# A decoder layer in split fp32: moving operands shifted by 128 bytes against the weights

## The chip, the cores and the metric

The kernel runs on one core of one Trainium2 chip. The metric is the device time of one execution in microseconds (us). Differences below about 0.2% of the time (4 us) can't be told from none.

## The reference

One layer of a hybrid decoder on 512 tokens of width 2,048, followed by a final norm:

```python
h = rms_norm(x, mix_norm_g)
p = h @ w_in                                   # 2048 -> 5136
out_a = conformer_conv_group(...)              # GLU, causal conv of width 31, LayerNorm, SiLU, 1024 x 1024
out_b = gated_deltanet_group(...)              # 8 value heads of 128, gated delta rule in chunks
x = x + concatenate([out_a, out_b]) @ w_out    # 2048 -> 2048
h = rms_norm(x, ffn_norm_g)
gate, up = split(h @ w_up, 2)                  # 2048 -> 2 x 5632
gate = causal_depthwise_conv(gate, ffn_conv_w) + ffn_conv_b
x = x + (silu(gate) * up) @ w_down             # 5632 -> 2048
return rms_norm(x, final_norm_g)
```

All inputs and outputs are float32.

## The kernel before

**Split products.** Activations lie transposed: 128 channels on the partitions, the 512 tokens along the free axis. The large products run in the type fp32r. Each operand is split in two tiles, a rounded high part (hi) and the remainder (lo). `mm3` (line 490) then issues three matmuls for a weight slice of 128 x 128: hi weights by hi activations, hi weights by lo activations, lo weights by hi activations. The stationary operand (`lhsT`, here called the weights) is loaded anew for every matmul, and TensorE loads the next one while the current moving operand (`rhs`, the activations) streams. Weights come from HBM in raw blocks of 128 x 1024 (`load_next`, line 450); ACT rounds 512 columns of one to hi (a cast), DVE subtracts to get lo (`split_piece`, line 460). A piece (hi, lo) holds four slices, 512 bytes apart within its 2,048 bytes.

**Stages.** The input projections come first, from the operands `xgh` and `xgl`, with the attention and convolution chains in between: small fp32 matmuls, transposes (`tr`), and the decay products `dec<-slgh,upper_r`. Then the mixer's output projections: `obh`, `obl` by half of `w_out`, `yh`, `yl` by the pointwise weights, `ah`, `al` by the other half. Then the FFN's up stage: 44 blocks, each of which computes the gate and up columns of 128 channels in seven products of half the tokens and half the depth instead of eight (a Strassen-like scheme). Its moving operands are `xb` (in the tiles XB) and `xt` (in XT), 256 columns each; DVE adds and subtracts raw weight blocks for it. Every second weight piece of the up stage is called `uhi`, `ulo`, the others `whi`, `wlo` (`cast`, line 1397). Last comes the down stage, with the stored FFN activations loaded again and split to `dh` and `dl`; its last tile runs in two halves of 256 tokens, with split weights in the tiles of `DT`.

**Order.** The order on every engine is written out by a planner in the program (class `Flow`): it keeps a clock for each engine from fixed costs of operations by shape, and starts tasks when their inputs are due by it. The address of a tile plays no part in it.

**Where tiles lie.** SBUF is given out from both ends. From the left: constants (`const`), the weight pool `wts` (three raw blocks, four hi and four lo pieces), then, one stage after another, the attention tiles, `xb`, `xt` and the down operands. From the right: the pool `pad` with one tile of 480 words that nothing uses (lines 314 and 315), then `acts1` and `acts2` (the split activations of the input and output projections), `conf`, and later in the same space `halves` (which prepares the up operands), `up` (line 1367: raw blocks `uraw`, `uhi`, `ulo`, and the small tiles of the FFN's output path) and `down2`. All tiles of weights and moving operands are multiples of 1 KB in size, so what lies ahead of the first tile of a side sets where all of them begin within 2 KB. `upper_r`, the weights of the decay products, is allocated after some small tiles and so begins elsewhere: at a multiple of 512 bytes.

Of the kernel before, what the change touches and what calls it, by code (L numbers as in the profile page):

```python
# [14 lines left out]
F32 = mybir.dt.float32  # L15
BF16 = mybir.dt.bfloat16
F32R = mybir.dt.float32r
# [4 lines left out]
P = 128  # L22
# [284 lines left out]
def tile_trunk(ctx: ExitStack, tc: tile.TileContext, xT, w_k, w_ba, w_m, pw, w_out, w_up, w_down, par_d, cst_d, out):  # L307
    nc = tc.nc
    fl = Flow(nc)
    V, ACT, POOL, SP = fl.vector, fl.scalar, fl.gpsimd, fl.sync  # L310
    ctx.enter_context(tc.manual_schedule(engines=ENGINES))
    cpool = ctx.enter_context(tc.tile_pool(name="const", bufs=1))
    wpool = ctx.enter_context(tc.tile_pool(name="wts", bufs=1))
    pad = ctx.enter_context(tc.tile_pool(name="pad", bufs=1, side="right"))
    pad.tile([P, 480], F32, name="pad")
    actx, a2ctx, cctx, gctx = [ExitStack() for _ in range(4)]
    apools = [
        c.enter_context(tc.tile_pool(name=n, bufs=1, side="right", reuse_waits="tile"))
# [9 lines left out]
    def nm(s):  # L328
        uid[0] += 1
        return f"{s}_{uid[0]}"  # L330

    def A(name, second=False):
        return fl.tile(apools[second], [P, T], F32R, "a", KT, nm(name))
# [116 lines left out]
    def load_next():  # L450
        i = len(raws)
        if i < (len(plan) if up_done else up_at + 3):
            src, n, step = plan[i]
            raw = fl.tile(wpool, [P, 1024], F32, "raw", 3, nm("wraw"))
            for o in range(0, n, n if i else step):
                e = o + (n if i else step)
                SP.dma_start(raw[:, o:e], src[:, o:e])
            raws.append(raw)
# [103 lines left out]
    def split_scaled(src, g, name, alloc):  # L562
        hi = alloc(name + "h")
        lo = alloc(name + "l")
        ACT.activation(out=hi, in_=src, func=AF.Copy, scale=g)
        V.scalar_tensor_tensor(out=lo, in0=src, scalar=g, in1=hi.bitcast(F32), op0=ALU.mult, op1=ALU.subtract)
        return hi, lo
# [97 lines left out]
    for k in range(KT):  # L665
# [4 lines left out]
        hi, lo = split_scaled(xs, mix_g[:, k : k + 1], "xg", lambda n: A(n, k >= KH))  # L670
# [566 lines left out]
    octx, xctx, tctx, uctx = [ExitStack() for _ in range(4)]  # L1237
# [21 lines left out]
    for m in range(NC):  # L1259
        ps = mtile(yhl)  # L1260
        hi, lo = A("ah"), A("al")
# [102 lines left out]
    fl.spawn(rms_stats(total[0], rstd2, 3.0), 6.0)  # L1364
    tctx.close()
    actx.close()
    upool = uctx.enter_context(tc.tile_pool(name="up", bufs=1, side="right", reuse_waits="tile"))

    def U(tag, bufs, w=T, dt=F32):
        return fl.tile(upool, [P, w], dt, tag, bufs, nm(tag))  # L1370

    def products_of(f):
        return PRODUCTS[0 if f == 0 else 2 if f == NF - 1 else 1]

    def up_products():


        blocks = {}

        def load(f, *names):  # L1380
            for n in names:
                if f == NF:
                    if n in (11, 22):
                        up_done.append(True)
                        load_next()
                    continue
                i, j = n // 10 - 1, n % 10 - 1
                if n in (11, 22):
                    t = fl.tile(wpool, [P, 1024], F32, "raw", 3, nm("wraw"))
                else:  # L1390
                    t = U("uraw", 3, 1024)
                SP.dma_start(t, w_up[2 * f + i][:, j * 1024 : (j + 1) * 1024])
                blocks[f, n] = t

        pend = deque()

        def cast(t, o):
            if o:
                hi, lo = U("uhi", 4, 512, F32R), U("ulo", 4, 512, F32R)
            else:  # L1400
                hi, lo = [fl.tile(wpool, [P, 512], F32R, n, 4, nm("w" + n)) for n in ("hi", "lo")]
            src = t[:, o * 512 : o * 512 + 512]
            ACT.copy(out=hi, in_=src)
            pend.append((src, hi, lo))

        def low():
            src, hi, lo = pend.popleft()
            V.tensor_tensor(out=lo, in0=src, in1=hi.bitcast(F32), op=ALU.subtract)
            pieces.append((hi, lo))

        def combine(out, a, b, op=ALU.subtract):
            V.tensor_tensor(out=out, in0=a, in1=b, op=op)

        blocks.update({(0, n): raws[up_at + i] for i, n in enumerate((11, 12, 22))})
        load(0, 21)

        def steps(f, a11, a22, a12, a21):

            def start():
                load(f + 1, 21)  # L1420
                if f:
                    load(f + 1, 11)

            def s1():
                combine(a22, a21, a22, ALU.add)

            def s2():
                combine(a22, a22, a11)
                load(f + 1, 22 if f else 11)

            def s3():
                combine(a21, a11, a21)

            def s4():
                combine(a12, a12, a22)

            if f in (0, NF - 1):
                start()
                urgent.extend((s1, s4))
                units = {  # L1440
                    "22": (a22, None, s1), "s1": (a22, s3, lambda: combine(a22, a22, a11)), "s3": (a21, None, None),
                    "s2": (a22, None, None), "11": (a11, None, lambda: load(NF, 22)), "12": (a12, None, s4),
                    "s4": (a12, None, None)}
                if f == 0:
                    units["s1"] = (a22, s3, s2)
                    units["s3"] = (a21, lambda: combine(a12, a12, a22), lambda: load(1, 12))
                    units["s2"] = (a22, None, lambda: load(1, 22))
            else:
                units = {
                    "11": (a11, start, None), "22": (a22, None, s1), "12": (a12, s3, None), "s1": (a22, None, s2),  # L1450
                    "s3": (a21, s4, lambda: load(f + 1, 12)), "s2": (a22, None, None if f else lambda: load(1, 22)),
                    "s4": (a12, None, None)}
            return [units[n] for n in products_of(f)]

        then, urgent = None, []
        for f in range(NF):
            units = steps(f, *[blocks.pop((f, n)) for n in (11, 22, 12, 21)])
            if f == 0:
                units = units[2:]
            for t, *acts in units:  # L1460
                for o in (0, 1):
                    if then in urgent:
                        low()
                        then()
                        then = None
                        yield
                    cast(t, o)
                    yield
                    if len(pend) > 1:
                        low()  # L1470
                    if then:
                        then()
                        yield
                    then = acts[o]
        low()
        load_next()
# [69 lines left out]
    for f in range(NF):  # L1546
# [7 lines left out]
        for n, w in enumerate(products_of(f)):  # L1554
            b, c, x = products[w]
            for k in range(KH):
                if k % 4 == 0:
                    hi, lo = pieces.popleft()
# [216 lines left out]
```

## Time and profile before

| | us |
|---|---|
| median of 3 runs | 2167.09 |
| lowest, highest | 2165.31, 2169.3 |
| the profiled execution's own time | 2161.55 |
| its span, first to last instruction | 2159.8 |

The profile shows one execution. Share of the span in which an engine is busy: TensorE's matmuls 99%, its weight loads (which run beside them) 89%, DVE 75%, ACT 44%, GpSimd 3%. The mean granted clock of TensorE is 0.997 of full speed. Matmuls overlap in the records: a record lasts from the issue to the last result, so its duration is longer than the time until the next one begins. The pace is read from the starts, or from a piece of the chain of waits, which gives the time and the number of matmuls that follow each other without a gap.

### The profile page before, as it was taken

To read this page: it belongs to the slowest core of one execution; us is meant where nothing else is said; L and a number is where in the kernel's file an instruction comes from. 1 tells how busy PE (TensorE), PEld (TensorE's weight loads), DVE (VectorE), ACT (ScalarE), POOL (GpSimd) and SP (SyncE) were. 2 spreads that over 40 slices of the span, in tenths; PEclk is the share of its full clock that TensorE was granted. 3 is DMA by queue.
4 is the path that set the end of the run, shared out by engine and by line. 5 is a ranking of instruction groups with operands and counts; after the bars stand their busy time and mean duration, and the time that the engine had idled before them with its cause. 6 is when DMAs were issued, how large, how long until landed. Compare 5 with 4: busy or idle time off the path is not lost.

```text
span 2159.8 us, 34257 instructions
## 1 busy us (share of the span) xinstructions
PE 2139.0 (99%) x13340; PEld 1926.0 (89%) x13340; DVE 1625.2 (75%) x2692; ACT 953.8 (44%) x1672; POOL 60.6 (3%) x59
## 2 busy tenths in 40 slices
PE   9999999999999999999999999999999999999997
PEld 7888888888788889999999999999999888888886
DVE  6899778888834789999999999999998633344344
ACT  5643544443333554554455455445445422233232
POOL 0310011000000000000000000000000000000000
PEclk9999999999999999999999999999999999999998
DMA  5252333333553533333343343343343733343333
GB/s 199 92 163 98 117 105 107 112 104 126 191 194 132 193 128 128 123 121 110 123 127 104 123 131 103 120 131 108 114 132 128 258 110 120 107 142 91 99 100 111
DMA packets 117618, 276.63 MB, mean 128 GB/s; under 512 B 23376, under 2 KB 36304, under 8 KB 117456
## 3 DMA queue, kind: packets, MB, share of 16 engines
q1 hardware_dynamic: 117312, 274.45, 39.5%
q8 instruction: 104, 1.70, 0.3%
q14 instruction: 58, 0.48, 0.1%
q10 hardware_dynamic: 144, 0.01, 0.0%
HBM read 240.33 MB, written 34.08 MB: 127 GB/s over the span
## 4 chain that ended last, share of the span: by engine, by line
PE 93%; DVE 3%; DMA 1%; issue 1%; ACT 0%; SPq 0%; POOLq 0%; POOL 0%; DVEq 0%; ACTq 0%
PE acc L99 49%; PE bz L99 11%; PE by L99 11%; PE bx L99 11%; PE bv L99 6%; PE tr L99 1%; DVE cacc L99 1%; DVE wlo L99 1%; PE e L99 1%; DMA wraw<-in_w_down_dram 0%; DMA yr<-scr_y 0%; PE pv L99 0%; PE ba L99 0%; PE po L99 0%; PE y L99 0%
## 5 line engine op out<-in xcount | busy, mean ns | idle before, releaser
L99 DVE TENSOR_TENSOR wlo<-wraw,whi 128x512 fp32r<-128x512 f32 (+1 forms) x616 | 414.3, 676 | 321.3 <-ACT whi L99 320.9
L99 ACT CAST whi<-wraw 128x512 fp32r<-128x512 f32 (+1 forms) x616 | 370.0, 606 | 579.1 <-PE acc L99 424.1
L99 PE MATMUL acc<-dh,wlo 128*128 128x512 f32 (+1 forms) x726 | 277.9, 383 | 0.8 <-DVE wlo L99 0.8
L99 PE MATMUL acc<-dh,whi 128*128 128x512 f32 (+1 forms) x726 | 278.0, 383 | 0.2 <-ACT whi L99 0.2
L99 PE MATMUL acc<-dl,whi 128*128 128x512 f32 (+1 forms) x726 | 277.9, 383 | 0.1
L99 PE MATMUL acc<-xgh,whi 128*128 128x512 f32 x640 | 260.2, 407 | 0.9 <-ACT xgh L99 0.9
L99 PE MATMUL acc<-xgl,whi 128*128 128x512 f32 x640 | 249.8, 390 | 0.6 <-DVE xgl L99 0.6
L99 PE MATMUL acc<-xgh,wlo 128*128 128x512 f32 x640 | 250.3, 391 | 0.0
L99 DVE SCALAR_TENSOR_TENSOR cacc<-u,par,cacc 128x495 f32<-128x495 f32 (+22 forms) x240 | 173.4, 741 | 1.7 <-ACT cacc L99 0.3
L99 PEld LDWEIGHTS acc<-dh,wlo 128*128 128x128 f32 x726 | 136.4, 188 | 27.8 <-DVE wlo L99 1.2
L99 PEld LDWEIGHTS acc<-dl,whi 128*128 128x128 f32 x726 | 136.4, 188 | 27.1 <-DVE dl L99 0.5
L99 PEld LDWEIGHTS acc<-dh,whi 128*128 128x128 f32 x726 | 136.4, 188 | 27.0 <-ACT whi L99 0.6
L99 ACT CAST uhi<-wraw 128x512 fp32r<-128x512 f32 x176 | 109.2, 621 | 104.2 <-PE by L99 64.8
L99 ACT CAST whi<-uraw 128x512 fp32r<-128x512 f32 x130 | 80.7, 621 | 151.6 <-DVE uraw L99 86.7
L99 PEld LDWEIGHTS acc<-xgh,wlo 128*128 128x128 f32 x640 | 120.1, 188 | 26.2
L99 DVE TENSOR_TENSOR ulo<-wraw,uhi 128x512 fp32r<-128x512 f32 x176 | 120.7, 686 | 28.8 <-ACT uhi L99 28.8
L99 PEld LDWEIGHTS acc<-xgh,whi 128*128 128x128 f32 x640 | 120.4, 188 | 24.3 <-ACT xgh L99 1.8
L99 PEld LDWEIGHTS acc<-xgl,whi 128*128 128x128 f32 x640 | 120.5, 188 | 23.3 <-DVE xgl L99 1.2
L99 PE MATMUL by<-xt,whi 128*128 128x256 f32 x704 | 130.5, 283 | 0.0
L99 PE MATMUL by<-xt,uhi 128*128 128x256 f32 x704 | 130.5, 283 | 0.0
L99 PEld LDWEIGHTS by<-xt,whi 128*128 128x128 f32 x704 | 109.8, 192 | 0.0
L99 PEld LDWEIGHTS by<-xt,uhi 128*128 128x128 f32 x704 | 109.8, 192 | 0.0
(277 smaller groups left out, 4722.0 us busy)
## 6 DMA issues: line engine op xcount, KB each, us to landing
wraw<-in_w_up_dram SPq DMA_DIRECT2D x89, 512.0 KB, 4.5
uraw<-in_w_up_dram SPq DMA_DIRECT2D x87, 512.0 KB, 4.4
wraw<-in_w_m_dram SPq DMA_DIRECT2D x74, 512.0 KB, 3.5
wraw<-in_w_down_dram SPq DMA_DIRECT2D x60, 512.0 KB, 3.6
wraw<-in_w_out_dram SPq DMA_DIRECT2D x32, 512.0 KB, 3.7
wraw<-in_w_down_dram SPq DMA_DIRECT2D x30, 384.0 KB, 3.4
scr_a<-fa SPq DMA_DIRECT2D x44, 256.0 KB, 2.1
dl<-scr_a SPq DMA_DIRECT2D x44, 256.0 KB, 5.1
```

What stands on the lines that cost most here:

```text
L99: return f(**kw) if not args else f(out, *args, **{k: v for k, v in kw.items() if k != "out"})
```

## The change

Three edits, all of them to where tiles lie. A pool `lpad` of one tile of 32 words (128 bytes) stands on the left, behind the weight pool, so every tile on the left after the weights begins 128 bytes later. The pad on the right shrinks from 480 to 448 words, so every tile on the right begins 128 bytes later too. In the up stage a further pad of 32 words and a pool `upw` stand on the right ahead of `up`: `uhi` and `ulo` get their tiles there and keep their start within 2 KB, and the rest of `up` lies below them.

```diff
@@ -311,8 +311,10 @@
     ctx.enter_context(tc.manual_schedule(engines=ENGINES))
     cpool = ctx.enter_context(tc.tile_pool(name="const", bufs=1))
     wpool = ctx.enter_context(tc.tile_pool(name="wts", bufs=1))
+    lpad = ctx.enter_context(tc.tile_pool(name="lpad", bufs=1))
+    lpad.tile([P, 32], F32, name="lpad")
     pad = ctx.enter_context(tc.tile_pool(name="pad", bufs=1, side="right"))
-    pad.tile([P, 480], F32, name="pad")
+    pad.tile([P, 448], F32, name="pad")
     actx, a2ctx, cctx, gctx = [ExitStack() for _ in range(4)]
@@ -1364,6 +1366,9 @@
     tctx.close()
     actx.close()
+    upad = uctx.enter_context(tc.tile_pool(name="upad", bufs=1, side="right"))
+    upad.tile([P, 32], F32, name="upad")
+    uwpool = uctx.enter_context(tc.tile_pool(name="upw", bufs=1, side="right", reuse_waits="tile"))
     upool = uctx.enter_context(tc.tile_pool(name="up", bufs=1, side="right", reuse_waits="tile"))
@@ -1396,7 +1401,7 @@
         def cast(t, o):
             if o:
-                hi, lo = U("uhi", 4, 512, F32R), U("ulo", 4, 512, F32R)
+                hi, lo = [fl.tile(uwpool, [P, 512], F32R, n, 4, nm("u" + n)) for n in ("hi", "lo")]
             else:
                 hi, lo = [fl.tile(wpool, [P, 512], F32R, n, 4, nm("w" + n)) for n in ("hi", "lo")]
```

## Rows read from the trace of the kernel before

**Rows 1.** Busy us by stage: window, length, PE, PEld, DVE, ACT, POOL, clock, DMA, GB/s.

```profile
60.00:545.00 485.00, 485.00 (x2492) 404.80 (x2491) 414.60 (x839) 225.62 (x421) 53.58 (x47) 1.00 0.36 115
...
601.30:769.80 168.50, 168.50 (x745) 139.53 (x744) 95.06 (x158) 74.00 (x131) 0.00 (x0) 1.00 0.51 169
769.80:1624.60 854.80, 852.03 (x7098) 851.59 (x7098) 783.43 (x1146) 427.44 (x725) 1.39 (x1) 1.00 0.37 119
...
1685.70:2137.80 452.10, 452.10 (x2035) 376.08 (x2036) 183.81 (x287) 137.80 (x240) 0.00 (x0) 1.00 0.38 117
```

**Rows 2.** The chain that ended last, shares of the span by engine.

```profile
PE 93%; DVE 3%; DMA 1%; issue 1%; ACT 0%; SPq 0%; POOLq 0%; POOL 0%; DVEq 0%; ACTq 0%
```

**Rows 3.** Groups of matmuls by form: out<-in, shape, count, busy us, mean ns, idle before.

```profile
L99 PE MATMUL acc<-dl,whi 128*128 128x512 f32 x682 | 265.5, 389 | 0.1
...
L99 PE MATMUL acc<-xgh,wlo 128*128 128x512 f32 x640 | 250.3, 391 | 0.0
...
L99 PE MATMUL by<-xt,whi 128*128 128x256 f32 x704 | 130.5, 283 | 0.0
...
L99 PE MATMUL acc<-obh,wlo 128*128 128x512 f32 x128 | 49.8, 389 | 0.0
...
L99 PE MATMUL acc<-ah,whi 128*128 128x512 f32 x128 | 49.8, 389 | 0.0
...
L99 PE MATMUL acc<-yh,whi 128*128 128x512 f32 x64 | 24.9, 389 | 0.0
```

**Rows 4.** Pieces of the chain of waits: start us, us, engine, tile, matmuls.

```profile
601.32 168.71 PE acc L99 x744
...
1005.46 5.76 PE by L99 x48
```

**Rows 5.** PE in order of time, around a pair of decay products: start us, us.

```profile
112.91 0.39 PE L99 MATMUL acc<-xgl,whi 128*128 128x512 f32 x1
113.13 0.40 PE L99 MATMUL acc<-xgh,wlo 128*128 128x512 f32 x1
113.37 0.39 PE L99 MATMUL dec<-slgh,upper_r 128*128 128x512 f32 x1
113.60 0.39 PE L99 MATMUL dec<-slgl,upper_r 128*128 128x512 f32 x1
113.83 0.40 PE L99 MATMUL acc<-xgh,whi 128*128 128x512 f32 x1
114.07 0.39 PE L99 MATMUL acc<-xgl,whi 128*128 128x512 f32 x1
```

**Rows 6.** PE in order of time, first and eleventh product after transposes.

```profile
162.09 0.40 PE L99 MATMUL acc<-xgl,whi 128*128 128x512 f32 x1
...
164.40 0.39 PE L99 MATMUL acc<-xgh,wlo 128*128 128x512 f32 x1
```

**Rows 7.** PE in order of time, bf16 warm-up, two overlapping windows.

```profile
4.50 1.03 PE L99 MATMUL warm<-wz 128*128 128x512 bf16 x4
...
4.93 0.59 PE L99 MATMUL warm<-wz 128*128 128x512 bf16 x2
```

**Rows 8.** PE in order of time, thirteen fp32 products of 64 columns.

```profile
238.22 1.61 PE L99 MATMUL e<-yt,DEm 128*128 128x64 f32 x13
```

**Rows 9.** The same products by tile: ns minimum/median/maximum, first and last start.

```profile
L99 PE MATMUL e<-yt,DEm x16: 218/275/275, 237.9 to 239.6; 128*128 128x64 f32 x16
```

**Rows 10.** Busy us in one block of the up stage, columns as in rows 1.

```profile
1005.46:1025.62 20.16, 20.16 (x170) 20.16 (x170) 18.50 (x29) 10.09 (x18) 0.00 (x0) 1.00 0.36 118
```

**Rows 11.** ACT and DVE in order of time at the start of the up stage.

```profile
775.37 1.23 DVE L99 TENSOR_TENSOR xt<-d,xt 128x1024 fp32r<-128x1024 f32 x1 [0.78 <-ACT xt L99]
...
776.59 0.61 ACT L99 CAST uhi<-wraw 128x512 fp32r<-128x512 f32 x1
...
783.18 0.37 ACT L99 COPY s<-bx 128x256 f32<-128x256 f32 x1
```

## The prediction

> **What bounds the kernel now.** I read the stage table first [rows 1]. In the input projections (60 to 545 us), the mixer's output projections (601 to 770), the FFN's up stage (770 to 1625) and its down stage (1686 to 2138) TensorE is busy for all but 3 us, with a granted clock of 1.00, which is the 2.4 GHz level. DVE, next after PE and its weight loads, is busy for 783 of 855 us in the up stage and less elsewhere. The chain of waits agrees: 93% of it is PE [rows 2]. So the time is the number of matmuls times the gap between their starts, and only a change in that gap can matter.
>
> The counts come from rows and code. Full-width products (512 moving columns): three per weight slice, so 3 x (682 + 640 + 128 + 128 + 64) = 4,926 [rows 3]. Half-width products of the up stage: 44 blocks x 7 products x 8 slices x 3 = 7,392, of which one operand pair makes 704 [rows 3]. Left out are 132 half-width products of the last down tile, 32 of the beta/decay projection and 16 of the decay matrices, discussed below.
>
> The gaps come from the chain [rows 4]. In the up stage 48 matmuls take 5.76 us: 120.0 ns each. In the output projections 744 take 168.71 us: 226.8 ns. The difference of 106.8 ns is for 256 more columns, 0.417 ns a column, so both shapes carry the same fixed part: 120.0 - 106.8 = 13 ns. 7,392 x 120.0 + 4,926 x 226.8 = 887 + 1,117 = 2,004 us of the 2,159.8 us span, and the fixed part alone is 12,318 x 13 ns = 160 us of it. That is what the change can touch.
>
> **The change, part by part.** The instructions, their order and their tiles' sizes stay: the planner's times in the code don't depend on addresses. No copy, load, wait or matmul is added or taken away.
>
> *Where the operands stand.* Summing the pools' sizes puts every weight tile 96 bytes past a multiple of 2 KB, on both sides of memory. A product's weights are a slice that starts 0, 512, 1,024 or 1,536 bytes into it. Moving tiles now also start 96 past, so modulo 512 bytes moving operand and weights start together. Afterwards the moving ones start at 224, the weights stay at 96. Exempt are the three groups above: the last down tile's split weights share a pool with the moving operands and shift with them, as do the padded beta/decay weights, and the decay products keep the distance they have.
>
> *What the distance does to the gap.* The trace of before has almost one distance only, so this is bounded from the nearest rows. Steps of 512 bytes are free: the 48 matmuls of one chain piece use slices at all four starts, at 120.0 ns throughout [rows 4]. A distance of 96 bytes is not free. The decay products take weights (upper_r) that start at a multiple of 512 while the stream beside them starts 96 later; from the last ordinary product before them to the second one after them four gaps take 0.94 us [rows 5], where four steady ones take 4 x 0.2268 = 0.907: 8 ns more each. The gap also isn't fixed at equal distance: after an interruption by transposes, ten gaps take 2.31 us [rows 6], 231 ns, before they settle at 227. So the fixed part depends on how the two streams meet. Ends of the range: above, 8 ns x 12,318 = +99 us. Below, two rows show shorter fixed parts: bf16 products of 512 columns, which repeat one set of weights, start 0.43 us apart for two [rows 7], 215 ns, 11.8 less; and fp32 products with only 64 moving columns but a full weight load each start (1.61 - 0.275) / 12 = 111 ns apart [rows 8, 9], so a load can come every 111 ns, 9 less than 120. That gives -(11.8 x 4,926 + 9 x 7,392) = -58 - 67 = -125 us. I take 0 between the ends, by the row nearest to it in kind: whatever in the pattern repeats must do so within 512 bytes and not within 32, since 96 is a multiple of 32 and costs something. That leaves 64, 128, 256 or 512, and at the first two a shift of 128 changes nothing.
>
> The Trainium skill ("TensorE: Matmul & The Clock Gate", Part 2, on loading the stationary operand) says that PE has two independent SBUF read ports and that loading the next weights does not steal read bandwidth from a running matmul; by it the change is worth 0. The rows of the decay products speak against that rule in general: there a different start of the weights goes with 8 ns a gap.
>
> *The split weights' own pool.* On the right uhi and ulo move to the top, over tiles of the attention and convolution operands, the rest of the up pool below them; the raw blocks stay. The first uhi is written at 776.59 us, behind whi on ACT [rows 11], and the tiles now under it had their last matmul before 770. The small tiles now over the buffers of halves are written from 783.18 us on, after the last xt, which DVE ends at 776.6 [rows 11]. Cost 0; if such a wait did come, it would be within the 3 us for which PE already stands idle there, and of that size.
>
> *Sum.* 2,161.6 us for the profiled execution (span 2,159.8 plus 1.8) + 0 + 0 = 2,161.6. The median of the three runs shown is 5.5 higher, 2,167.1, so I forecast 2,167.
>
> **The rivals.** *Faster: the streams stop meeting.* For it: the fixed part is the same 13 ns at 256 and 512 columns, as a collision that happens once per weight load would be, and equal starts are where two readers should collide most. Against it: no row at another distance has a shorter gap with weights of this type. In full it is worth -125 us by the rows, 2,042; but DVE would then have to do its 18.50 us of a block [rows 10] while PE needs 168 x 111 ns = 18.6 us, so the up stage would stand at DVE's edge and I hold about 110 of it for reachable: 2,057. Half a collision less gives 2,112.
>
> The skill's page gives a gap of columns / 2.4 plus about 2.5 ns for a warm stream (same page, "Back-to-back issue gap"). By it an estimate would be 10.8 ns x 12,318 = 133 us less, 2,034; the measured 120 and 226.8 ns already stand 11 ns above that rule.
>
> *Slower: the new distance is a worse meeting.* One mechanism: the stream begins 128 bytes ahead of the weights and runs into them later in the load, as in the decay products. Its place is every ordinary product, its price 4 ns a gap (as after an interruption: 231 - 226.8) to 8 ns (decay products), so +52 to +99 us: 2,219 to 2,266. It decides if the pattern repeats at 256 or 512 bytes. For it: 96 bytes, the only distance near 128 in the trace, costs. Against it: these are single passages, and a long stream settles, as it does after each interruption.
>
> *The pads do nothing.* No instruction uses the pad tiles; if they took no space, addresses would stay and so would the time. The same number as the forecast.
>
> **How the numbers follow.** Four repeats are possible and two give no change, so about half, less a tenth, because a cost of 8 ns at 96 bytes looks like a coarse pattern: 0.40 for no change, which counts as within 0.2% (4 us, what a measurement of this kernel can tell from none). The other 0.60 I split 0.34 faster, 0.26 slower: of all starts an equal one looks likeliest to collide, but the one other distance seen costs. Range: the faster cases spread from -4 to -110 us, the slower from +4 to +99; down to 2,090 holds some 0.24 of the first, up to 2,240 some 0.19 of the second, with 0.40 together about 0.8. The likeliest case alone is 2,163 to 2,171.
>
> **What would show it.** Right: 48 matmuls of the up stage in 5.76 us and full-width gaps of 227 ns, as now. Faster would show as pieces under 5.7 us with DVE busy for nearly all of the up stage; slower as pieces over 5.8 us. If whi and uhi products differ, the side of the memory counts and not the distance. If the gaps stand but the time moves, a wait has come at the up stage's start. I am wrong if the gap at 128 bytes is not that at 0.

## The result and the profile after

The changed kernel takes 2,180.5 us (median of 4 runs, 2,178.9 to 2,182.9) where the kernel before takes 2,166.3 (4 runs): a ratio of 1.0066 with a 95% interval of 1.0053 to 1.0078, so 0.66% or 14 us **slower**. The profiled execution is one of 2,178.9 us with a span of 2,177.0, against 2,161.6 and 2,159.8 before. The forecast was no change, 2,167.

The stage table of the kernel after, the same windows and columns as [rows 1]:

```profile
60.00:545.00 485.00, 485.00 (x2463) 400.00 (x2462) 411.27 (x834) 220.34 (x410) 54.35 (x47) 1.00 0.35 113
...
601.30:769.80 168.50, 168.50 (x730) 136.51 (x729) 90.58 (x157) 71.24 (x126) 1.30 (x1) 1.00 0.52 170
769.80:1624.60 854.80, 851.98 (x7123) 849.03 (x7122) 789.23 (x1159) 433.14 (x735) 1.38 (x1) 1.00 0.38 121
...
1685.70:2137.80 452.10, 452.10 (x1940) 363.70 (x1939) 180.15 (x281) 136.53 (x236) 0.00 (x0) 1.00 0.39 120
```

Read the number of matmuls in the same stretch of time. TensorE is as busy as before and its granted clock is the same 1.00. Yet in the stages with 512 columns fewer products fit (2,463 for 2,492, 730 for 745, 1,940 for 2,035; the last stretch also begins a little earlier in the work), and in the up stage with its 256 columns **more** do (7,123 for 7,098). The two widths moved in opposite directions.

The chain's shares by engine, and its pieces in the same three stages (start us, us, engine, tile, matmuls), against [rows 2] and [rows 4]:

```profile
PE 98%; DVE 1%; issue 0%; DMA 0%; ACT 0%; SPq 0%; POOLq 0%; POOL 0%; DVEq 0%
```

```profile
610.34 164.76 PE acc L99 x709
...
1016.20 3.80 PE by L99 x32
...
1689.94 410.20 PE acc L99 x1758
```

164.76 us / 709 = 232.4 ns for a full-width gap, where [rows 4] had 226.8; 3.80 us / 32 = 118.75 ns for a half-width gap, where it had 120.0. The down stage's piece gives 233.3. The groups by form, against [rows 3], show the same two signs in the mean ns of one matmul (389 to 395, 283 to 281):

```profile
L99 PE MATMUL acc<-dl,whi 128*128 128x512 f32 x682 | 269.4, 395 | 0.0
L99 PE MATMUL by<-xt,whi 128*128 128x256 f32 x704 | 129.2, 281 | 0.0
```

Measured from the start of one product to the start of the next over all products of a kind, the change comes out as follows. Down stage: 2,046 gaps from 226.7 to 233.3 ns, +13.7 us. Input projections: from 228.3 to 232.6 on average (that stage is interrupted often, so its gaps never were all 226.7), +7.9. Output projections: some 226.8 to 232.6, +3.9 with the gaps around interruptions in the sum. Up stage: 120.0 to 118.67, -9.8. Together +15.7, against 17.3 between the two profiled executions and 14 between the medians. The 132 half-width products of the last down tile, whose weights moved along with them, take 16.0 us in both traces, and products with `whi` and with `uhi` have the same 281 ns now, so it is not the side of the memory that counts.

Nothing new waits at the up stage's start. All waits of TensorE between 769 and 800 us after (engine, tile, releaser: us, times, longest), which were 1.9 and 0.9 before:

```profile
PE bv L99 <- ACT whi L99: 2.0, 1, 2.0
PE bv L99 <- DVE wlo L99: 0.9, 1, 0.9
```

### The profile page after: what moved, and what is told of

Its sections match the earlier page's. It is cut to its first block, busy times and chain, and to the rows that moved or that the text cites. A ratio compares the mean times of both kernels' runs of the same rounds, so it can differ in the third digit from the quotient of the medians.

```text
span 2177.0 us, 34257 instructions
## 1 busy us (share of the span) xinstructions
PE 2156.9 (99%) x13340; PEld 1918.8 (88%) x13340; DVE 1625.7 (75%) x2692; ACT 955.8 (44%) x1672; POOL 61.4 (3%) x59
## 4 chain that ended last, share of the span: by engine, by line
PE 98%; DVE 1%; issue 0%; DMA 0%; ACT 0%; SPq 0%; POOLq 0%; POOL 0%; DVEq 0%
PE acc L99 53%; PE by L99 12%; PE bz L99 11%; PE bx L99 11%; PE bv L99 6%; PE tr L99 1%; PE e L99 1%; PE pv L99 0%; PE ba L99 0%; PE po L99 0%; PE y L99 0%; PE psn L99 0%; PE pk L99 0%; DMA dl<-scr_a 0%; PE pq L99 0%
```

## The experiments

**A map of starts.** The layer's work is replaced by streams of 48 products for each pair of starts, first full width, then half width, on tiles that stay in SBUF, with the same three products per slice as in the layer:

```python
    for w, m in SHIFTS:
        for cols, tag in ((512, "full"), (256, "half")):
            ps = ps_pool.tile([P, 512], F32, tag="ps", bufs=4, name=f"{tag}_{L[w]}{L[m]}")
            for k in range(16):
                t, j = k // 4 % 4, k % 4
                hi = wts[:, w * STEP + t * 512 + j * 128 :][:, 0:P]
                lo = wts[:, w * STEP + (t + 4) * 512 + j * 128 :][:, 0:P]
                xh = mov[:, m * STEP + 2 * (k % 4) * 512 :][:, 0:cols]
...
                for n, (lw, rx) in enumerate(((hi, xh), (hi, xl), (lo, xh))):
```

> This kernel leaves the layer out: TensorE alone runs streams of fp32r products on resident tiles, three per weight slice as in the layer (hi weights by hi moving, hi by lo, lo by hi), 48 in a row of 512 columns and 48 of 256 for each pair of starts (weights, moving) within 512 bytes, both in steps of 32 bytes: 256 pairs. Place theory (where each operand itself begins counts): the map has no constant diagonals; equal starts give 120.0 and 226.7 ns only at some places such as 96, and other gaps at 224. Distance theory (only the moving start minus the weights' start counts): every diagonal is one number, 120.0 and 226.7 at distance 0, 118.7 and 232 to 233 at 128. If starts repeat every 128 bytes, rows four steps apart are equal.

The chain of this run, one line per stream of 48 (16 steps of 32 bytes for each start, the last two letters being those of the weights and of the moving operand: "ae" is a distance of 128):

```profile
36.66 5.75 PE half_aa L342 x48
...
70.20 5.44 PE half_ac L342 x48
...
92.61 11.20 PE full_ae L342 x48
103.81 5.70 PE half_ae L342 x48
...
159.97 10.89 PE full_ai L342 x48
170.86 5.75 PE half_ai L342 x48
```

Each line divided by 48 is a gap. The steady gaps, by distance (moving start minus weights' start) modulo 256 bytes:

| distance | 0 | 32 | 64 | 96 | 128 | 160 | 192 | 224 |
|---|---|---|---|---|---|---|---|---|
| 512 columns, ns | 226.7 | 233.3 | 228.8 | 233.4 | 233.3 | 234.3 | 233.3 | 233.3 |
| 256 columns, ns | 120.0 | 116.7 | 113.3 | 120.0 | 118.8 | 118.8 | 113.3 | 118.3 |

A line at 256 bytes ("ai") repeats the one at 0, and pairs with the same distance at other places have the same gap but for a few streams. One kind of exception turned out to matter: of the 64 half-width streams at distances 64 and 192, eight stood at 117.8 and not at 113.3. So the gap goes by the distance and repeats after 256 bytes, a shift of 128 costs full width 6.6 ns and gives half width 1.2, much as in the changed kernel (6.6 and 1.3). The place by itself counts for nothing.

**bf16 operands** in the same map, with the layer's work left out in the same way (wts and mov are bf16 tiles and the step is 16 elements).

> As grid, this kernel leaves the layer out, and weights and moving operands are bf16: the same 256 pairs of starts in steps of 32 bytes. If a collision of two 4-byte streams is the cause (each at the full rate), 2-byte streams leave room and all pairs stand at one gap, 213 to 216 ns for 512 columns and 107 to 110 for 256. If every reload of weights costs a fixed 13 ns, then 227 and 120 everywhere. If starts collide with bf16 too, the gaps differ by diagonal, with a repeat of 256 bytes or of 128.

```profile
36.44 5.24 PE half_aa L342 x48
...
88.48 10.36 PE full_ae L342 x48
98.84 5.24 PE half_ae L342 x48
```

But for the opening stream, all 256 pairs stand at 215.8 ns (512 columns) and 109.2 ns (256). Of the two types only the 4-byte one shows an effect of the distance.

**Both operands shifted.** The pads of the change without the right side's own pool, and so that weights and moving operands move by 128 bytes together.

```diff
+    lpad = ctx.enter_context(tc.tile_pool(name="lpad", bufs=1))
+    lpad.tile([P, 32], F32, name="lpad")
     pad = ctx.enter_context(tc.tile_pool(name="pad", bufs=1, side="right"))
-    pad.tile([P, 480], F32, name="pad")
+    pad.tile([P, 448], F32, name="pad")
```

Here `lpad` stands ahead of the weights' pool, where the change has it behind.

> Weights and moving operands all begin 128 bytes later than in the kernel before: distance 0 as there, place 224 in place of 96. Distance theory: 120.0 ns in the up stage, 226.7 ns for full width, the time of before within 0.2% (2,166 us). Place theory: half width as in the last down tile of the changed kernel, which stood at 224 on both sides, 119.9 ns on average in a cycle of 117 to 124; full width some 229 to 233 ns, so 5,000 x 2 to 6 ns = 10 to 30 us slower than before.

2,163.7 us (10 runs) against 2,165.5: ratio 0.9997, 0.9988 to 1.0007. Its chain has the line of [rows 4] again, 5.76 us for 48:

```profile
1005.82 5.76 PE by L99 x48
```

Pads and places cost nothing that shows; the distance does.

**Half of the change.** Only xt, the moving operand of 4,224 half-width products, goes to distance 128.

```diff
+    xpad = xctx.enter_context(tc.tile_pool(name="xpad", bufs=1))
+    xpad.tile([P, 32], F32, name="xpad")
     xpool = xctx.enter_context(tc.tile_pool(name="operands_t", bufs=1, reuse_waits="tile"))
```

> Only the xt operands of the up stage begin 128 bytes later; everything else stands as before. If each product's gap hangs on its own operands' starts alone, the 4,224 xt products take 118.7 ns and the rest 120.0 and 226.7, so 4,224 x 1.33 = 5.6 us less than before, 2,160 to 2,161. Rival (the shorter half-width gap of the changed kernel comes from the whole layout, or is lost because xb and xt products alternate and disturb each other): xt products at 120 or above, no gain or a small loss, 2,166 to 2,172.

2,158.4 us (9 runs) against 2,165.5: ratio 0.9969, 0.9960 to 0.9979, 7 us faster. In its chain the products with xt (by) take 5.70 / 48 = 118.75 ns, those with xb (bv) 2.87 / 24 = 119.6, with 120.0 once settled:

```profile
1001.03 2.87 PE bv L99 x24
1003.90 5.70 PE by L99 x48
```

Half width alone gains, about by the amount of the map, 4,224 x 1.3 ns = 5.6 us. This version beats both kernels, and with the sums by stage above it shows that the change's loss is all in full width.

**Distance 64**, where the map has its best half-width gap: everywhere (the change with pads of 16 words for 32), and in the up stage's operands alone:

```diff
+    bpad = ctx.enter_context(tc.tile_pool(name="bpad", bufs=1))
+    bpad.tile([P, 16], F32, name="bpad")
     bopool = ctx.enter_context(tc.tile_pool(name="operands_b", bufs=1, reuse_waits="tile"))
...
+                dpad = ctx.enter_context(tc.tile_pool(name="dpad", bufs=1))
+                dpad.tile([P, 48], F32, name="dpad")
                 dleft = ctx.enter_context(tc.tile_pool(name="down1", bufs=1, reuse_waits="tile"))
```

> The change with 64 bytes in place of 128 in all three pads. By the map (gap set by the distance modulo 256 bytes, and by the width): 113.3 ns in the up stage, 228.8 at full width. Sum against before: -6.7 ns x 7,392 = -49 us, +2.1 x 4,926 = +10 us: 39 us less, about 2,127. Rival: DVE holds the up stage back (18.5 us of work a block; 168 x 113.3 = 19.0 us), gaps there of 115 ns or more with waits on wlo or ulo, 2,140 or above. Rival: the map's gaps are those of idle neighbours and don't carry over, then anything between 2,160 and 2,180.

> xb and xt begin 64 bytes later, everything of the other stages stays at distance 0, but for the down operands that get a former place of xb (297 x 3 products at distance 64). Map: -6.7 ns x 7,392 = -49 us, +2.1 x 891 = +2 us: 47 us less, about 2,118 to 2,119. Rival (DVE's edge): the same up stage as all64 but slower than 113.3 ns a product; then up64 keeps 8 us on all64 and both lose the same.

Everywhere: 2,156.0 us (5 runs), ratio 0.9953 (0.9940 to 0.9967). Up stage alone: 2,153.6 us (5 runs), ratio 0.9943 (0.9931 to 0.9956). Both beat the kernels, and both miss their forecasts, by 29 and 35 us. The chain of the second:

```profile
1002.54 2.83 PE bv L99 x24
1005.37 5.65 PE by L99 x48
```

5.65 us / 48 = 117.7 ns, where the map has 113.3. Between 800 and 1,600 us TensorE waits for nothing in either trace, so it isn't another engine's edge.

**Distance 192** everywhere (the change with pads of 48 words).

> The change with 192 bytes in all three pads, which is 64 less than the repeat of 256. By the map: 113.3 ns in the up stage as at +64, but 233.3 at full width: -49 + 6.6 x 4,926 = -49 + 33 = 17 us less than before, about 2,149. Rival (only the size of the distance counts, not its sign): as all64, 2,127.

Its ten runs lie at two times and nowhere between: four at 2,145.4 to 2,147.0 and six at 2,174.7 to 2,178.2. The granted clock is 0.995 to 0.997 in all ten, so it does not part them. The 30 us between them are close to 7,392 x (117.75 - 113.3) = 33. The profiled execution is one of the longer ones, and its chain holds both rhythms:

```profile
800.08 5.44 PE by L99 x48
805.52 1.36 PE bx L99 x12
806.88 0.89 PE statb L99 x8
807.77 1.42 PE bx L99 x12
809.18 2.83 PE bz L99 x24
...
820.49 5.65 PE by L99 x48
```

Up to the statistics of the next norm (four fp32 products, eight matmuls in the trace) a gap is 5.44 / 48 = 113.3 ns; behind them it is 117.8, to the end of the stage. The clock is 1.00 on both sides of the switch, so I formed a second theory: **at distances 64 and 192 a half-width stream has two rhythms, and keeps the one in which it was entered**.

**Entries.** The layer's work is left out; streams of 60 half-width products stand behind such statistics, with other products in between.

```python
        for dist, tag in ((64, "d"), (192, "e"), (0, "z")):
...
                short(f"stat_{L}", 4)
                if count:
                    stream(f"kick_{L}", cols, d2 if d2 >= 0 else dist, count)
                stream(f"half_{tag}{L}", 256, dist, 60)
```

> The layer's work is left out: PE alone runs streams of 60 half-width products at distances 64, 192 and 0 (weights at 96), each behind four fp32 products with 128 columns as the up stage has them at its statistics, with 0 to 24 other products in between (full width, 128 columns, half width at another distance); each sequence stands three times. Theory of two rhythms: at distances 64 and 192 a half-width stream keeps the rhythm in which it is entered, 113.3 or 117.8 ns, for all of its 60 products; which one follows from what stands before it, the same in all three repeats, and some of the 16 entries give each; at distance 0 every entry settles at 120.0 within some three products. Rival, that 117.8 ns in the whole kernel comes from the other engines' traffic in memory: with PE alone every entry at 64 and 192 gives 113.3. Rival, that it is the fp32 statistics that always lead to 117.8: all entries directly behind them give 117.8 and those with other products in between 113.3.

```profile
46.69 0.89 PE stat_a L342 x8
47.58 7.07 PE half_da L337 x60
...
82.19 6.80 PE half_de L337 x60
...
185.93 6.82 PE half_ea L337 x60
```

Once settled, each stream is at 113.33 or at 117.8 and stays. At distance 64, 5 of the 16 entries gave 113.33 in all three repeats, one in two of three, the others 117.8; directly behind the statistics always 117.8. At 192, 12 of 16 gave 113.33, the entry directly behind the statistics among them. At distance 0 all 48 streams settled at 120.0. TensorE was alone here, so other engines' traffic isn't what makes 117.8.

A second set of entries had products of 128 columns at the stream's own distance in between (0 to 6, 8, 10, 12; five repeats) and 1 to 6 at distance 0.

> As the first run of entries (the layer's work is left out), five repeats, and between the fp32 products and the half-width stream stand 0 to 12 products of 128 columns at the stream's own distance (which is what one gets by issuing a product of the stream in two halves), or 1 to 6 of them at distance 0. Theory of two rhythms: none in between gives 117.8 at distance 64 and 113.3 at 192 again; among the other numbers some give 113.3 at distance 64, each the same in at least four of five repeats, with no order by number. Rival, that any 128-column products in even number mend it: 2, 4, 6, 8, 10 and 12 all give 113.3. If every number at the stream's own distance gives 117.8, such a split can't be used in the whole kernel.

Most entries again gave one rhythm in all five repeats, with no order by number, even or odd: at 64, of 15 entries two always gave 113.33 (two or three products at distance 0, as in the first set); at 192, eleven. But one expectation missed: directly behind the statistics at 64 it was 117.8 once and 113.33 four times. The once came after the opening full-width stream, the four after a half-width stream at 192, so what ran before the statistics counts too. Two more entries at 64, with two and with three products at the stream's own distance in between, also stood otherwise in the first repeat than in the other four (117.8 against 113.33, and the reverse).

**Another entry in the whole kernel.** Up stage alone at distance 192 (the pads of the up-stage version with 48 words and 16), then the same with the first product behind the statistics issued in two halves, and that split at distance 64.

```diff
     def matmul(self, out, lhsT, rhs, start=True, stop=True):
+        if self.split and rhs.shape[-1] == 256:
+            self.split -= 1
+            for h in (0, 128):
+                self.tensor.matmul(
+                    out=out[:, h : h + 128], lhsT=lhsT, rhs=rhs[:, h : h + 128], start=start, stop=stop)
+            return
...
             fl.matmul(ps2[:, blk(i)], lhsT=r[:, i : i + 1].to_broadcast([P, P]), rhs=ident)
+        fl.split = 1 if lag else 0
```

> Only the up stage's moving operands (xb, xt) and the down tiles in the same pool stand at distance 192, all others at 0 or 256. Theory of two rhythms: each run lands at one of two times and at none between. The up stage at 117.8 ns: 7,300 gaps less 2.2 ns = -16, the down stage's 891 products at 192 +6, so some 2,156 us; at 113.3 ns: -49 + 6, some 2,123 us. The entry decides, at the four fp32 statistics products near 794 us; alone they led to 113.3 at 192 in all eight tries of the two entry kernels, so I expect 2,123 in more than half of the runs. Rival, that 113.3 can't be held in a full kernel beside the other engines: all runs at 2,156.

> As up192, and the first product behind the statistics is issued in two halves of 128 columns (one more weight load, some 0.1 us). Theory of two rhythms: this is another entry, which gave 113.3 at distance 192 in five of five tries of the second entry kernel; some 2,123 us in most runs, and the share of runs at 2,156 is another one than in up192. Rival: no difference to up192, each run by chance.

> As the earlier run with distance 64 in the up stage alone, which stood at 117.8 ns in all of its runs, but with the first product behind the statistics issued in two halves. The second entry kernel gave 113.3 in four of five tries for this entry and 117.8 in one. Theory of two rhythms: a part of the runs at some 2,122 us, where the earlier kernel had none of five; the rest at 2,154. If all stay at 2,154, the split is no remedy at this distance, and entry alone is not shown to be the cause in the full kernel.

| version | runs, us | ratio to before |
|---|---|---|
| 192 | 2,153.8, 2,156.6, 2,158.0, 2,158.3 | 0.996 (0.9946 to 0.9975) |
| 192, one product split | 2,124.5, 2,125.6, 2,126.2, 2,154.7 | 0.985 (0.979 to 0.991) |
| 64, one product split | 2,150.7, 2,151.6, 2,152.4, 2,153.9 | 0.994 (0.992 to 0.996) |

The chain without the split:

```profile
780.18 1.50 PE stat L99 x8
...
791.75 1.36 PE bx L99 x12
793.11 0.89 PE statb L99 x8
794.00 1.42 PE bx L99 x12
795.41 2.83 PE bz L99 x24
```

and with it, and the busy time of that version in 800 us of the up stage (columns as in rows 1):

```profile
780.91 0.79 PE stat L99 x8
...
789.93 1.41 PE bx L99 x12
791.34 0.89 PE statb L99 x8
792.23 1.49 PE bx L99 x13
793.72 2.72 PE bz L99 x24
...
1005.88 2.72 PE bx L99 x24
```

```profile
800.00:1600.00 800.00, 800.00 (x7061) 800.00 (x7060) 774.96 (x1139) 416.93 (x716) 0.00 (x0) 1.00 0.39 124
```

Without the split the stream goes from 113.3 ns before the statistics (1.36 / 12) to 117.9 behind them (2.83 / 24), as at distance 192 everywhere; that all four runs had the longer time missed the forecast of 2,123 us in more than half of them. With it the stream goes the other way, from 117.5 (1.41 / 12) to 113.3 (2.72 / 24), and holds that for the more than 7,200 products that remain. The operands stand at the same addresses in both, so in the whole kernel too one and the same stream has both rhythms and switches where it is interrupted. This version is the fastest of the study: three of four runs at 2,124 to 2,126, 40 us under the kernel before. In its trace the up stage is 47 us shorter than in the kernel before and the down stage 10 us longer. The fourth run, at 2,154.7, fits the other rhythm, but its trace wasn't taken.

That the split is what turned the rhythm is not shown by these two versions. Without any split, four of the ten runs at distance 192 everywhere had the short time. And the two traces differ before the split can act: the stream comes to the statistics at 113.3 ns in one and at 117.5 in the other, and an earlier set of statistics (`stat`, eight matmuls) ran at a granted clock of 0.50, the 1.2 GHz level, in the first (1.50 us) and 1.00 in the second (0.79 us). The clock behind these statistics, without the split and with it (window, length, PE, clock, DMA, GB/s):

```profile
782.00:783.00 1.00, 1.00 (x7) 0.50 0.00 0
```

```profile
782.00:783.00 1.00, 1.00 (x11) 1.00 0.00 0
```

A rival therefore stands: at 192 the statistics may turn whichever rhythm they meet, and what picks the first one may be what happens at the stage's start.

At 64 the times hide what the split did. Pieces of the chain, of TensorE and of its weight loads in that trace:

```profile
785.05 4.25 PE by L99 x36
```

```profile
794.32 0.39 PE L99 MATMUL bz<-xb,whi 128*128 128x256 f32 x2
...
807.92 0.39 PE L99 MATMUL by<-xt,whi 128*128 128x256 f32 x2
```

```profile
808.33 0.19 PEld L99 LDWEIGHTS by<-xt,wlo 128*128 128x128 f32 x1 [0.21 <-DVE wlo L99]
...
810.07 0.19 PEld L99 LDWEIGHTS by<-xt,ulo 128*128 128x128 f32 x1 [0.26 <-DVE ulo L99]
```

```profile
811.52 2.83 PE bx L99 x24
```

Before the statistics a gap is 118 ns (4.25 / 36). Behind the split product it is 113.3 ns (13.60 us for 120 products), as four of five tries of the small kernel had let expect. Then two weight pieces from DVE come 0.2 to 0.3 us late, and behind these waits the stream is at 117.9 (2.83 / 24) and stays near that to the end of the stage. So a short wait can cost the rhythm too. The other three runs of this version also had the longer time; they weren't traced.

Taken together, the rhythm behind these statistics was 117.8 ns in all four traces without a split (both versions at 64, both at 192) and 113.3 in both traces with one. That favours the split as the cause. But in those four the clock was at 0.50 for a while at the earlier statistics and in these two it was not, so the two are not parted. Which rhythm an entry gives I can't forecast.

## Why the prediction was wrong

**Right: the bound, the counts, what costs nothing.** PE made up 98% of the chain after (93% before), 7,392 and 4,926 products were what the change acted on, and the gap alone moved. The pool of the split weights and the pads cost 0 as forecast: the two waits at the up stage's start are 2.0 and 0.9 us for 1.9 and 0.9, and shifting everything together left the time at 0.9997.

**The step that failed: "I take 0 between the ends, by the row nearest to it in kind".** That wasn't a row. It was a count of possible repeats (64, 128, 256, 512), two of which happened to give no change. The map says 256 bytes: 128 is half a period, as far from equal starts as one can get, and 256 was one of the two repeats under which the prediction itself held the slower rival for right. The row that did measure another distance was the decay products at 96 bytes [rows 5], +8 ns a gap. The map has +6.7 at 96 and +6.6 at 128, so for full width that row was the price, and the rule to go by the nearest measured row would have found it: 4,926 x 8 = +39 us as a bound, and +25.5 as measured (13.7 + 7.9 + 3.9).

**The second failure: one fixed part for both widths.** From 120.0 - 106.8 = 13 ns and 226.8 - 213.3 = 13 ns I concluded that both widths pay the same and would move together. The equality held at distance 0 alone. At 128 full width goes to 20 ns over its columns and half width to 12. So the two rivals were each right for one width and wrong for the other. *Slower* put 4 to 8 ns on every ordinary product; it was 4 to 7 ns on the 4,926 of full width only, +25.5 us where it said +52 to +99. *Faster* took up to 9 ns off; it was 1.3 off the 7,392 of half width, -9.8 us. That equal starts collide most holds in the map for 256 columns (120.0 ns at 0 and 96, the most of any distance) and fails for 512, whose best is at 0. The sum, +15.7, lies well inside the range and in the chance of 0.26; that it is so small is luck, for two moves that the prediction did not see apart cancel in part. What to look for was right in part: the up stage's pieces fell to 5.70 us, just at the mark for "faster", while the whole got slower, a case that the list didn't have. The last sign named there, a gap at 128 bytes that is not that at 0, came.

**The ends.** bf16 products [rows 7] were no floor for these operands: their gap doesn't depend on the starts at all, and the full-width stream's best is 226.7, which it already had. For half width the floor of 111 ns from fp32 products [rows 9] was near: the best rhythm is 113.3. DVE's edge, at which I cut the faster rival to 110 us, is near too: in the fastest version DVE is busy for 775 of 800 us and PE still waits for nothing, while in the split version at 64 weights from DVE that came 0.2 to 0.3 us late ended the short rhythm.

**The rules cited, against the trace.** By the Trainium skill ("TensorE: Matmul & The Clock Gate", Part 2), loading weights takes no read bandwidth from a running matmul. For bf16 the map agrees: no pair of starts differs. For these 4-byte operands what the prediction drew from it, no effect of the starts, does not hold: 113.3 to 120.0 ns, or 226.7 to 234.3, by the starts alone. Whether it is read bandwidth that is lost, no run shows. The Trainium skill's same page, section "Back-to-back issue gap", gives columns / 2.4 + 2.5 ns for the gap of an isolated warm product, by estimate 215.8 and 109.2 ns. The bf16 map, streams with new weights for every product, measured just these. No 4-byte stream of 256 columns at 2.4 GHz came under 113.3 ns.

**What stays open.** The records show that the gap goes by the distance, not what inside the chip makes it. A meeting of two 4-byte read streams fits the bf16 map and the lack of any effect of place, but it is argued, not shown. Open is also what in an entry picks the rhythm, and whether the split or the clock at the stage's start made the fastest version.

## What to carry to other kernels

When the bound is the gap between matmuls, measure the gap of each operand width by itself against the starts of both operands before moving any of them: here one shift made 256 columns faster and 512 columns slower. With 4-byte operands keep full-width streams at a distance of 0 modulo 256 bytes, and try 64 and 192 for half-width ones. Where two executions of one kernel lie at two times, look in a trace for the place where the gap switches, and read the gaps even where the time did not change: a rhythm can be won and lost again within one stage.

## What was not expected of the hardware

A stream of equal matmuls can have two stable rhythms: at distances 64 and 192, 113.33 and 117.8 ns for 256 columns. At 192 a whole kernel held each of them for over 7,000 products. They switched at an interruption of 0.9 us, and at 64 once at waits of 0.2 to 0.3 us. In the whole kernel that is 30 us.

The fixed part vanishes at the lower clock level. In the run at distance 192 the clock is at 0.50 for a while, after TensorE's two waits of 2.0 and 0.9 us at the up stage's start. The stretch and its clock, and the first and last product of 15 gaps in it:

```profile
796.00:799.00 3.00, 3.00 (x16) 0.50 0.00 0
```

```profile
796.20 0.41 PE L99 MATMUL bz<-xt,wlo 128*128 128x256 f32 x1
...
799.40 0.32 PE L99 MATMUL bz<-xt,ulo 128*128 128x256 f32 x1
```

3.20 us / 15 = 213.3 ns, which is 256 columns at 1.2 GHz and nothing over. In the kernel with both operands shifted, at distance 0, nine gaps at a clock of 0.50 take 1.92 us (776.93 to 778.85), 213.3 ns as well. At 2.4 GHz such products have 7 to 13 ns over their columns.
